# A decoder trunk on one core: float32 weights for two feature blocks, modulation blocks given out anew, a last norm by halves

## The chip, the cores and the metric

One core of a Trainium2 chip runs the whole program. The metric is device time in microseconds (us) of one execution. The engines are PE (TensorE, matmuls), DVE (VectorE), ACT (ScalarE), POOL (GpSimd) and SP (SyncE, which here only issues DMAs); each works through a queue of its own.

## What is computed

One layer on 256 tokens of width 2048, in float32:

```python
mod = (silu(c) @ w_ada + b_ada)
sh1, sc1, g1, sh2, sc2, g2 = jnp.split(mod, 6, axis=-1)
h = rms_norm(x, norm_mix) * (1.0 + sc1) + sh1
x = x + g1 * hybrid_mixer(h, w_in, w_out, ...)
h = rms_norm(x, norm_ffn) * (1.0 + sc2) + sh2
x = x + g2 * conv_glu_ffn(h, w_ffn_up, ..., w_ffn_down)
return rms_norm(x, norm_final)
```

The mixer runs retention, RWKV-7 and block-sparse attention side by side on slices of h @ w_in and multiplies the joined result by w_out. The MLP is 2 x 5632 wide, with a causal convolution of width 3 ahead of its gate.

## The kernel before

**Tiles.** Features lie on the partitions and the 256 tokens along the free axis. Every weight matrix is cut into 128x128 blocks; a block is the stationary operand of a matmul and a 128x256 feature block of the input the moving one. For exactness weights and inputs are each split into a high and a low part (`hi`, `lo`; of the inputs `hhi`, `hlo`), and a block costs three matmuls, L1226 (hi by hi), L1227 (hi by the input's low part) and L1228 (lo by hi). Eight blocks are a chunk, 24 matmuls; there are 400 chunks: "in" (w_in) 0 to 103, "out" (w_out) 104 to 135, "up" (w_ffn_up) from 136, "down" (w_ffn_down) from 312. The chunk is the only unit in which weights reach PE.

**Stream.** `stream_items` is one list of 1 MB pieces in the order in which they are used: two chunks of weights, or one modulation block (128 rows of w_ada). `pump` issues their DMAs on SP in this order, as soon as one of 3 raw slots (5 at the start: two "extra" ones) is free; later weights may also take memory that the mixer gave back, as many as `LEAD` allows at that chunk. `convert_until` takes the pieces in the same order, two chunks ahead of PE (`AHEAD`). A weight chunk is copied to `hi` by ACT (L465) and its `lo` is formed by DVE (L466); `hi` and `lo` have three buffers each (`CONVB`), so a conversion can be at most that far ahead of PE. A modulation block is one DVE instruction (L420): it multiplies the raw slot in place by `cb` (silu of c on all partitions) and sums each row into one column of `mod`; L422 or L428 adds the bias. So a raw slot with a modulation block comes free by DVE.

**Modulations.** There are 96 such blocks. Shift and gain of the first norm (32) stand among the first feature blocks of "in", g2 (16) among the last stages. The 48 between them (g1, then shift and gain of the second norm) are given out by `LATE_ADA`, in this order: the last piece of "in", four pieces of "out" of five 1 MB pieces each (the last has one), three pieces of "up". Inside each piece they are spread evenly.

```python
parts = [(win[cut[-1]:], 0)] + [(out[n:n + 5], 0) for n in range(0, 20, 5)]
parts += [(up[cut_up[g]:cut_up[g + 1]], 2) for g in range(3)]
for n, (part, after) in zip(LATE_ADA, parts):
    n_part = len(part) - after
    stream_items += mix(part[:n_part], late[:n]) + part[n_part:]
    late = late[n:]
```

`UP_BEGUN` says how many pairs of "up" tiles are begun with the first 4, 8 and 12 feature blocks of the second norm's output, before the rest of it is known.

**Order.** One Python loop over the chunks emits all instructions: conversion, hooks, the chunk's matmuls, evacuations, and `TASKS` steps of the mixer's generators. A scheduler then fixes the order of each engine's queue at build time; at run time each engine goes through its own queue and waits where an operand is not there. So a DVE instruction that is put ahead of a `lo` delays this `lo`.

**First norm.** x comes in four pieces, ACT squares them (L370), DVE adds (L374 to L376), PE averages over features (L379, `ms`), and `norm_bcast` forms m (L386), its inverse root by a bit trick and three Newton steps on DVE (`rsqrt`, L240 to L245), and spreads it by PE (L390, `rs`). `h_tile` then makes each feature block: xn (L446), `hhi` (ACT, L447), `hlo` (L448). Eight S tiles and eight W tiles of "in" take the first four feature blocks in pairs (`pair`).

**Second norm.** `evac_out` (L1066) adds gate times product to x, block by block; ACT squares it (L1079), POOL adds the squares to `acc` (L1080; DVE for the last block). `ffn_start` averages (L1084, `nps`), takes the root and multiplies; meanwhile the first eight pairs of "up" run on unnormed inputs (`xghi`, `xglo`), and `scale_early` corrects them afterwards (L1120).

**Last norm.** `evac_down` (L1167) and `norm_acc` do the same for the output, and `finish` multiplies all 16 blocks by `rs` on DVE (L1175) in five pieces and stores each from SP (L1176).

## Time and profile before

| | |
|---|---|
| times of three runs | 1270.31, 1273.58, 1273.6 us (median 1273.58) |
| profiled execution | 1276.42 us, its span 1274.6 us |
| busy: PE, DVE, ACT, POOL | 1227.2 us (96%), 1030.1 us (81%), 651.2 us (51%), 42.6 us (3%) |
| granted TensorE clock, mean | 0.987 |
| HBM read | 316.83 MB, 250 GB/s over the span |
| chain that ended last, by engine | PE 83%, DVE 7%, issue 5%, ACT 2%, DMA 1%, POOL 1% |

Span is from the first to the last instruction; some 2 us lie around it. Busy times are sums over instructions, matmuls being pipelined: the time from one matmul's start to the next is what a chunk costs, and it is read from the starts. A wait of PE that no other work fills is time lost, since PE has something to do in nearly every other microsecond. Averages over the span say little of single places; the stages below are cut at the places where the kind of work changes.

### The profile page before, as it was taken

Reading aid. Unit: us, or ns where it says so; the run is one execution under the profiler, and the core shown is the slowest. Engines: PE = TensorE matmul, PEld = TensorE weight load, DVE = VectorE, ACT = ScalarE, POOL = GpSimd, SP = SyncE. Lnnn points to the kernel's source line nnn. Section 1 sums busy time; section 2 is a strip of 40 time slices with the busy share of each in tenths; the row PEclk is TensorE's granted clock in tenths of the full one; section 3 lists DMA queues with packets and bytes.
Section 4 is the critical chain, followed back from the end, with each engine's and each line's share of the span. In section 5 each row is a group of like instructions: output and inputs, shape, how many; then the busy total and the mean of one; then the engine's idle time right before and its main releaser. Section 6 shows DMA issues by size and latency. Waiting matters only on the chain.

```text
span 1274.6 us, 25479 instructions
## 1 busy us (share of the span) xinstructions
PE 1227.2 (96%) x10608; PEld 1205.3 (95%) x10608; DVE 1030.1 (81%) x1607; ACT 651.2 (51%) x1043; POOL 42.6 (3%) x41
## 2 busy tenths in 40 slices
PE   5899999999999999899999999999999999999995
PEld 4899999989998889899999999999999999999995
DVE  6988989989988589899887999899866766666444
ACT  4354443756434534566555666666555544444441
POOL 0000000000000000600000000000000000000000
PEclk7999999999999999999999999999999999999998
DMA  9899877876654569677984565565655677767551
GB/s 387 343 365 334 341 300 273 300 261 229 230 179 166 199 240 412 241 281 254 357 308 172 193 223 200 197 232 198 216 196 188 228 263 271 285 250 288 196 199 67
DMA packets 49940, 320.58 MB, mean 252 GB/s; under 512 B 5536, under 2 KB 6048, under 8 KB 15776
## 3 DMA queue, kind: packets, MB, share of 16 engines
q1 hardware_dynamic: 48528, 315.10, 67.5%
q0 software_dynamic: 1008, 3.67, 0.8%
q8 instruction: 83, 1.36, 0.4%
q14 instruction: 33, 0.27, 0.1%
q10 hardware_dynamic: 288, 0.17, 0.1%
HBM read 316.83 MB, written 2.10 MB: 250 GB/s over the span
## 4 chain that ended last, share of the span: by engine, by line
PE 83%; DVE 7%; issue 5%; ACT 2%; DMA 1%; POOL 1%; DVEq 0%; ACTq 0%; POOLq 0%
PE mm L1226 25%; PE mm L1227 24%; PE mm L1228 24%; DVE raw L420 3%; DVE lo L466 2%; ACT hi L465 1%; PE pair L1228 1%; PE xx L787 1%; PE pair L1227 1%; PE pair L1226 1%; POOL acc L1080 1%; DMA dec<-dec 1%; PE akv L800 1%; DMA x<-xT 1%; PE cb L406 0%
## 5 line engine op out<-in xcount | busy, mean ns | idle before, releaser
L466 DVE TENSOR_TENSOR lo<-raw,hi 128x1024 fp32r<-128x1024 f32 x400 | 489.1, 1225 | 164.5 <-ACT hi L465 161.5
L465 ACT CAST hi<-raw 128x1024 fp32r<-128x1024 f32 x400 | 419.0, 1049 | 387.3 <-PE mm L1227 335.1
L1226 PE MATMUL mm<-hhi,hi 128*128 128x256 f32 x2016 | 561.0, 278 | 0.5 <-DVE proj L501 0.5
L1228 PE MATMUL mm<-hhi,lo 128*128 128x256 f32 x2016 | 559.8, 278 | 1.1 <-DVE lo L466 1.1
L1227 PE MATMUL mm<-hlo,hi 128*128 128x256 f32 x2016 | 559.8, 278 | 0.0
L1228 PEld LDWEIGHTS mm<-hhi,lo 128*128 128x128 f32 x2016 | 378.9, 188 | 2.4 <-DVE lo L466 1.9
L1226 PEld LDWEIGHTS mm<-hhi,hi 128*128 128x128 f32 x2016 | 379.4, 188 | 1.4 <-DVE proj L501 0.7
L1227 PEld LDWEIGHTS mm<-hlo,hi 128*128 128x128 f32 x2016 | 378.9, 188 | 0.9 <-issue 0.2
L420 DVE SCALAR_TENSOR_TENSOR raw<-raw,cb 128x2048 f32<-128x2048 f32 x96 | 219.8, 2290 | 6.1 <-DMA raw<-w_ada 4.9
L1226 PE MATMUL mm<-ghi,hi 128*128 128x256 f32 x704 | 194.8, 277 | 0.0
L1227 PE MATMUL mm<-glo,hi 128*128 128x256 f32 x704 | 194.8, 277 | 0.0
L1228 PE MATMUL mm<-ghi,lo 128*128 128x256 f32 x704 | 194.8, 277 | 0.0
L1226 PEld LDWEIGHTS mm<-ghi,hi 128*128 128x128 f32 x704 | 132.2, 188 | 0.0
L1228 PEld LDWEIGHTS mm<-ghi,lo 128*128 128x128 f32 x704 | 132.2, 188 | 0.0
L1227 PEld LDWEIGHTS mm<-glo,hi 128*128 128x128 f32 x704 | 132.1, 188 | 0.0
L1226 PE MATMUL mm<-mxhi,hi 128*128 128x256 f32 x256 | 72.9, 285 | 2.4 <-DVE x L1066 2.4
L1227 PE MATMUL mm<-mxlo,hi 128*128 128x256 f32 x256 | 73.1, 286 | 0.0
L1228 PE MATMUL mm<-mxhi,lo 128*128 128x256 f32 x256 | 72.5, 283 | 0.0
L1080 POOL TENSOR_TENSOR acc<-acc,nsq 128x256 f32<-128x256 f32 x28 | 36.6, 1309 | 792.9 <-ACT nsq L1079 792.5
L1226 PEld LDWEIGHTS mm<-mxhi,hi 128*128 128x128 f32 x256 | 49.0, 191 | 3.4 <-DVE x L1066 2.6
L1226 PE MATMUL pair<-hhi,hi 128*128 128x256 f32 x160 | 45.1, 295 | 6.9 <-ACT hi L465 5.0
L1228 PEld LDWEIGHTS mm<-mxhi,lo 128*128 128x128 f32 x256 | 48.8, 191 | 1.4 <-DVE lo L466 0.7
(292 smaller groups left out, 1281.8 us busy)
## 6 DMA issues: line engine op xcount, KB each, us to landing
raw<-w_ada SPq DMA_DIRECT2D x96, 1024.0 KB, 5.1
raw<-w_up SPq DMA_DIRECT2D x67, 1024.0 KB, 4.8
raw<-w_in SPq DMA_DIRECT2D x52, 1024.0 KB, 6.1
raw<-w_down SPq DMA_DIRECT2D x44, 1024.0 KB, 4.9
raw<-w_up SPq DMA_DIRECT2D x42, 512.0 KB, 8.4
raw<-w_out SPq DMA_DIRECT2D x18, 512.0 KB, 9.9
raw<-w_out SPq DMA_DIRECT2D x7, 1024.0 KB, 4.8
x<-xT SPq DMA_DIRECT2D x4, 512.0 KB, 5.6
```

Source lines behind the costliest of these rows:

```text
L420: V.scalar_tensor_tensor(raw, raw, 1.0, cb, op0=OP.mult, op1=OP.mult, accum_out=m)
L465: S.copy(flat(hi), src)
L466: V.tensor_tensor(flat(lo), src, flat(hi).bitcast(F32), op=OP.subtract)
L787: return PE.matmul(pe[e][:, o:o + 128], (Bt, Kt)[i][pb, f, sl], (At, Rt)[n][pb, f, sl], start=True, stop=True)
L800: PE.matmul(ps[:, 128 * i + 64 * e:128 * i + 64 * e + 64], xv[:, e, 128 * i:128 * i + 128], vT[:, h, 64 * hd:64 * hd + 64], start=True, st ...
L1080: (V if t == NF - 1 else G).tensor_tensor(norm["acc"], norm["acc"], sq, op=OP.add)
L1226: PE.matmul(ps, whi[:, j], hi, start=first and not (two and t % 2), stop=False, skip_group_check=two)
L1227: PE.matmul(ps, whi[:, j], lo, start=False, stop=False, skip_group_check=two)
L1228: PE.matmul(ps, wlo[:, j], hi, start=False, stop=last, skip_group_check=two)
```

## The change

- `PLAIN = 2`: the weights of the first two feature blocks are used in float32 as they lie in the raw slot. Their 4 casts and 4 `lo` are left out, and a block is one float32 matmul (L1291) with a float32 copy of the normed input (`plain`, ACT) in place of three.
- `spin`: matmuls on a zeroed tile whose result nobody reads, 12, 10, 18 and 6 of them, around the four steps of the first norm.
- First norm: the squares come behind the `cb` matmuls in the program; `rsqrt` does one Newton step on DVE and two on ACT (column by column). The modulation blocks may start only behind the first Newton step (`issue_after(seed...)`), later ones behind one of the first four xn; the first `lo` likewise.
- `LATE_ADA` becomes (8, 7, 5, 4, 0, 8, 8, 8), `UP_BEGUN` (18, 9, 7). The last piece of "in" has 10 modulation blocks fewer, "out" has 16 in place of 8, "up" 24 in place of 22.
- The load of x for the residual waits on g1's column 7 in place of its last one.
- The norms' last block: the residual sum and the squares go by halves, and the squares go to PE directly (`norm["last"]`) in place of DVE's addition to `acc`. In `finish` POOL multiplies the last four blocks by an SBUF copy of `rs` and ACT's queue stores them.
- `SMALL_PAD` 16 becomes 8, the last entry of `LEAD` (186, 1) becomes (188, 1).

```diff
-UP_BEGUN = (22, 8, 4)
+UP_BEGUN = (18, 9, 7)
+SPIN = (12, 10, 18, 6)
+PLAIN = 2
-LATE_ADA = (18, 3, 3, 2, 0, 7, 7, 8)
+LATE_ADA = (8, 7, 5, 4, 0, 8, 8, 8)
-CONST_PAD, SMALL_PAD = 32, 16
+CONST_PAD, SMALL_PAD = 32, 8
-LEAD = ((116, 0), (145, 8), (152, 6), (164, 4), (172, 3), (186, 1))
+LEAD = ((116, 0), (145, 8), (152, 6), (164, 4), (172, 3), (188, 1))
...
-        for _ in range(3):
+        if E is S:
+            half = tiny("rsh", w)
+            V.tensor_scalar(half, x, -0.5, None, op0=OP.mult)
+        for _ in range(3 if E is V else 1):
...
+        if E is S:
+            for i in range(w):
+                y1, a1 = y[:, i:i + 1], a[:, i:i + 1]
+                for _ in range(2):
+                    S.activation(a1, y1, AF.Square)
+                    S.activation(a1, a1, AF.Identity, scale=half[:, i:i + 1], bias=three_half)
+                    S.activation(y1, y1, AF.Copy, scale=a1)
...
+    def spin(n):
+        for _ in range(n):
+            tc.keep_in_program_order(PE.matmul(spin_bank[:, 0:128], idle[:, 0, 0:128], idle[:, 1, 0:128], start=True, stop=True))
...
-    ms = mean_square(XT)
+    spin(SPIN[0])
...
-    norm_scale(ms, "mix")
+    spin(SPIN[1])
+    ms = mean_square(XT)
+    norm_scale(ms, "mix", E=S, before=lambda: spin(SPIN[2]))
+    spin(SPIN[3])
...
-        V.scalar_tensor_tensor(raw, raw, 1.0, cb, op0=OP.mult, op1=OP.mult, accum_out=m)
+        with tc.issue_after((seed[:1] + scaled[:4])[-1]):
+            V.scalar_tensor_tensor(raw, raw, 1.0, cb, op0=OP.mult, op1=OP.mult, accum_out=m)
...
+            elif it[1] == "in" and it[2] < PLAIN:
+                chunks.extend((it[1], 16 * it[2] + 8 * half, flat_raw, None)
...
-                V.tensor_tensor(flat(lo), src, flat(hi).bitcast(F32), op=OP.subtract)
+                with tc.issue_after(scaled[:4][-1]):
+                    V.tensor_tensor(flat(lo), src, flat(hi).bitcast(F32), op=OP.subtract)
...
-            S.copy(x[:, 0, 0:1], mod["g1"][:, NF - 1:])
+            S.copy(x[:, 0, 0:1], mod["g1"][:, 7:8])
...
+            for h in range(2):
+                S.activation(sq[:, 128 * h:128 * h + 128], x[:, 128 * h:128 * h + 128], AF.Square)
+            norm["last"] = sq
...
+        for n, x in enumerate((norm["acc"], norm["last"])):
+            for h in range(2):
+                PE.matmul(ps[:, h:h + 1], x[:, 128 * h:128 * h + 128], K("mean"), start=(n == 0 and h == 0),
+                          stop=(n == 1), skip_group_check=True)
...
+        S.copy(rs_copy, rs[:, 0:T])
+        for a, b in ((0, 1), (1, 4), (4, 8), (8, 12)):
...
+        for a in (12, 14):
+            for t in (a, a + 1):
+                G.tensor_tensor(x1[3][:, t % 4], x1[3][:, t % 4], rs_copy, op=OP.mult)
+            S.dma_start(A["outT"][:, a:a + 2, :], x1[3][:, a % 4:a % 4 + 2])
...
+            if wlo is None:
+                PE.matmul(ps, whi[:, j], plain[0][:, k], start=first and not (two and t % 2), stop=last,
+                          skip_group_check=two)
+                continue
```

New line numbers: L420 is L455, L422 and L428 are L457 and L463, L466 is L510, L1066 is L1114, L446 and L448 are L481 and L487, L1120 is L1178, L240 to L245 are L246 to L254.

The change also moves DVE's instructions among the chunks. In the rows below a name is the tile written, then `<-` and the tiles read; `raw` with a column of `mod` is a modulation block, `lo` the low part of a weight chunk.

**First place: DVE in "out".** Before, from U (a tile of the RWKV recurrence) over the `lo` of chunks 115, 116 and 117:

```order
L953 TENSOR_TENSOR U<-u_5188,R_3478 32x512
L466 TENSOR_TENSOR lo_5438<-raw_5201,hi_5437 128x1024
L436 TENSOR_TENSOR mxlo_5183<-mix_rwkv_4909,mxhi_5182 128x4x128
L976 TENSOR_TENSOR sb_4906<-sp_5082,pcs_5194 64x4x64 x2
L1066 SCALAR_TENSOR_TENSOR x_4746<-mm_5397,mod_g_162,x_4746 128x256
L466 TENSOR_TENSOR lo_5482<-raw_5315,hi_5481 128x1024
L953 TENSOR_TENSOR U<-u_5252,R_3478 32x512
L1066 SCALAR_TENSOR_TENSOR x_4746<-mm_5467,mod_g_162,x_4746 128x256
L466 TENSOR_TENSOR lo_5511<-raw_5315,hi_5510 128x1024
```

With the change, three modulation blocks (raw_5399, raw_5433, raw_5472) stand between the `lo` of chunk 117 and these rows, which go on to the `lo` of chunk 118:

```order
L997 TENSOR_TENSOR U<-u_5142,R_3440 32x512
L1114 SCALAR_TENSOR_TENSOR x_4692<-mm_5531,mod_g_221,x_4692 128x256
L471 TENSOR_TENSOR mxlo_5137<-mix_rwkv_4855,mxhi_5136 128x4x128
L463 TENSOR_TENSOR mod_ffn_shift<-mod_ffn_shift,vec 128x1
L455 SCALAR_TENSOR_TENSOR raw_5505,mod_ffn_gain<-raw_5505,cb 128x2048
L1020 TENSOR_TENSOR sb_4852<-sp_5036,pcs_5148 64x4x64 x2
L457 SCALAR_TENSOR_TENSOR mod_ffn_gain<-mod_ffn_gain,bias_225,vec 128x1
L455 SCALAR_TENSOR_TENSOR raw_5576,mod_ffn_shift<-raw_5576,cb 128x2048
L997 TENSOR_TENSOR U<-u_5206,R_3440 32x512
L510 TENSOR_TENSOR lo_5516<-raw_5401,hi_5515 128x1024
```

Before, at most one modulation block stood between two `lo` here; now five stand between two, with the evacuation of mm_5531, whose last matmul is the last of chunk 117, among them.

**Second place: DVE in the second norm.** Before, from m on:

```order
L386 TENSOR_SCALAR m_6282<-nps_6279 128x2
L240 TENSOR_SCALAR rsy_6284<-m_6282 128x2
L241 TENSOR_SCALAR rsy_6284<-rsy_6284 128x2
L466 TENSOR_TENSOR lo_6334<-raw_5729,hi_6333 128x1024
L243 SCALAR_TENSOR_TENSOR rsa_6285<-rsy_6284 128x2
L420 SCALAR_TENSOR_TENSOR raw_6369,mod_ffn_gain<-raw_6369,cb 128x2048
L244 TENSOR_TENSOR rsa_6285<-rsa_6285,m_6282 128x2
L466 TENSOR_TENSOR lo_6376<-raw_5795,hi_6375 128x1024
L245 SCALAR_TENSOR_TENSOR rsy_6284<-rsa_6285,rsy_6284 128x2
L422 SCALAR_TENSOR_TENSOR mod_ffn_gain<-mod_ffn_gain,bias_166,vec 128x1
L243 SCALAR_TENSOR_TENSOR rsa_6285<-rsy_6284 128x2
L244 TENSOR_TENSOR rsa_6285<-rsa_6285,m_6282 128x2
```

With the change, from m on:

```order
L413 TENSOR_SCALAR m_6260<-nps_6255 128x2
L463 TENSOR_TENSOR mod_ffn_shift<-mod_ffn_shift,vec 128x1
L455 SCALAR_TENSOR_TENSOR raw_6245,mod_ffn_gain<-raw_6245,cb 128x2048
L246 TENSOR_SCALAR rsy_6262<-m_6260 128x2
L510 TENSOR_TENSOR lo_6312<-raw_5923,hi_6311 128x1024
L247 TENSOR_SCALAR rsy_6262<-rsy_6262 128x2
L457 SCALAR_TENSOR_TENSOR mod_ffn_gain<-mod_ffn_gain,bias_225,vec 128x1
L252 SCALAR_TENSOR_TENSOR rsa_6263<-rsy_6262 128x2
L510 TENSOR_TENSOR lo_6360<-raw_5996,hi_6359 128x1024
L253 TENSOR_TENSOR rsa_6263<-rsa_6263,m_6260 128x2
L455 SCALAR_TENSOR_TENSOR raw_6353,mod_ffn_shift<-raw_6353,cb 128x2048
L254 SCALAR_TENSOR_TENSOR rsy_6262<-rsa_6263,rsy_6262 128x2
```

Before, one modulation block stood in the whole chain from m to the last Newton step; now four do (two more follow these rows in the same pattern: a modulation block, a Newton row, a `lo`).

**Third place: DVE behind that chain.** Before, behind the `lo` of chunk 143:

```order
L466 TENSOR_TENSOR lo_6516<-raw_5960,hi_6515 128x1024
L448 SCALAR_TENSOR_TENSOR hlo_6465<-xn_6466,mod_ffn_shift,hhi_6464 128x256
L448 SCALAR_TENSOR_TENSOR hlo_6465<-xn_6480,mod_ffn_shift,hhi_6464 128x256
L466 TENSOR_TENSOR lo_6558<-raw_6099,hi_6557 128x1024
L1120 TENSOR_TENSOR up_6415<-up_6415,rs_ffn 128x1024
L1120 TENSOR_TENSOR up_6510<-up_6510,rs_ffn 128x1024
L466 TENSOR_TENSOR lo_6593<-raw_6100,hi_6592 128x1024
```

With the change, from the chain's last row on (the `lo` of chunk 143 is just ahead, that of chunk 144 comes 20 rows below the first one here):

```order
L254 SCALAR_TENSOR_TENSOR rsy_6262<-rsa_6263,rsy_6262 128x2
L463 TENSOR_TENSOR mod_ffn_shift<-mod_ffn_shift,vec 128x1
L455 SCALAR_TENSOR_TENSOR raw_6606,mod_ffn_gain<-raw_6606,cb 128x2048
L481 SCALAR_TENSOR_TENSOR xn_6349<-x_4689,mod_ffn_gain,rs_ffn 128x256
L481 SCALAR_TENSOR_TENSOR xn_6365<-x_4686,mod_ffn_gain,rs_ffn 128x256
L1178 TENSOR_TENSOR up_6306<-up_6306,rs_ffn 128x1024
L487 SCALAR_TENSOR_TENSOR hlo_6348<-xn_6349,mod_ffn_shift,hhi_6347 128x256
L457 SCALAR_TENSOR_TENSOR mod_ffn_gain<-mod_ffn_gain,bias_225,vec 128x1
L481 SCALAR_TENSOR_TENSOR xn_6369<-x_4686,mod_ffn_gain,rs_ffn 128x256
L455 SCALAR_TENSOR_TENSOR raw_6691,mod_ffn_shift<-raw_6691,cb 128x2048
L455 SCALAR_TENSOR_TENSOR raw_6764,mod_ffn_gain<-raw_6764,cb 128x2048
L487 SCALAR_TENSOR_TENSOR hlo_6364<-xn_6365,mod_ffn_shift,hhi_6363 128x256
```

Before, no modulation block stood between the `lo` of chunks 143 and 145; now three stand between those of chunks 143 and 144, and with them the feature blocks of the second norm, of which chunk 144 is the first to need any.

## Rows read from the trace of the kernel before

**Rows 1.** Windows: us; busy (instructions) of PE, PEld, DVE, ACT, POOL; clock, DMA share, GB/s.

```profile
23.67:56.53 32.86, 27.47 (x193) 26.57 (x194) 29.11 (x37) 10.76 (x14) 0.00 (x0) 0.87 0.90 358
...
221.90:392.60 170.70, 167.00 (x1338) 156.82 (x1337) 159.61 (x353) 92.26 (x202) 3.66 (x5) 1.00 0.66 234
392.60:536.10 143.50, 135.89 (x1293) 127.06 (x1292) 117.24 (x210) 68.84 (x132) 19.42 (x16) 0.98 0.68 261
536.10:595.00 58.90, 57.53 (x494) 57.17 (x493) 55.82 (x81) 38.04 (x88) 3.95 (x3) 1.00 0.69 250
595.00:1259.70 664.70, 664.70 (x5853) 664.70 (x5852) 497.92 (x687) 351.97 (x486) 15.36 (x14) 1.00 0.64 229
```

**Rows 2.** PE's waits: who was waited for, us in total, times, longest.

```profile
PE rs L390 <- DVE rsy L245: 9.5, 2, 7.1
...
PE pair L1226 <- ACT hi L465: 5.0, 2, 3.3
...
PE mm L1226 <- DVE x L1066: 2.4, 1, 2.4
...
PE nps L1084 <- DVE mod_ffn_shift L428: 1.3, 1, 1.3
```

**Rows 3.** Timeline of DVE, first norm: start, duration, instruction, wait ahead of it.

```profile
13.72 2.29 DVE L420 SCALAR_TENSOR_TENSOR raw<-raw,cb 128x2048 f32<-128x2048 f32 x1 [0.93 <-ACT cb L408]
...
15.93 0.15 DVE L386 TENSOR_SCALAR m<-ms 128x2 f32<-128x2 f32 x1
```

**Rows 4.** Timeline of PE, the six float32 matmuls of L675 that stand together.

```profile
243.73 1.46 PE L675 MATMUL a<-rwm,wua 96*128 96x256 f32 x6
```

**Rows 5.** Timeline of DVE in "out", end of an RWKV step.

```profile
457.44 2.28 DVE L420 SCALAR_TENSOR_TENSOR raw<-raw,cb 128x2048 f32<-128x2048 f32 x1
...
459.65 0.60 DVE L1011 SCALAR_TENSOR_TENSOR mix_rwkv<-yt,vec,rwm 128x128 f32<-128x128 f32 x2
...
461.74 0.67 DVE L953 TENSOR_TENSOR U<-u,R 32x512 f32<-32x512 f32 x1
462.34 1.20 DVE L466 TENSOR_TENSOR lo<-raw,hi 128x1024 fp32r<-128x1024 f32 x1
...
464.97 0.48 DVE L1066 SCALAR_TENSOR_TENSOR x<-mm,mod_g,x 128x256 f32<-128x256 f32 x1
```

**Rows 6.** Timeline of PE, the same place and a later one.

```profile
457.58 0.66 PE L1006 MATMUL yt<-cst,yc 128*128 128x128 f32 x4 [0.25 <-DVE yc L1002]
458.17 1.06 PE L948 MATMUL u<-sb,m 128*32 128x128 f32 x8
...
473.81 0.68 PE L921 MATMUL sp<-U,bT 32*64 32x64 f32 x16
```

**Rows 7.** Timeline of DVE, second norm, from m to the last Newton step.

```profile
541.43 0.16 DVE L386 TENSOR_SCALAR m<-nps 128x2 f32<-128x2 f32 x1 [0.69 <-PE nps L1084]
...
543.12 2.28 DVE L420 SCALAR_TENSOR_TENSOR raw<-raw,cb 128x2048 f32<-128x2048 f32 x1
...
547.70 0.16 DVE L245 SCALAR_TENSOR_TENSOR rsy<-rsa,rsy 128x2 f32<-128x2 f32 x1
```

**Rows 8.** Window behind PE's wait of 2.4 us at 524.8, columns as in rows 1.

```profile
527.40:530.90 3.50, 3.50 (x16) 3.50 (x17) 2.41 (x5) 1.58 (x3) 2.21 (x2) 0.51 0.57 239
```

**Rows 9.** DMA issues of the page: KB each, median us from issue to landing.

```profile
raw<-w_ada SPq DMA_DIRECT2D x96, 1024.0 KB, 5.1
```

**Rows 10.** DVE's waits for modulation data: us in total, times, longest.

```profile
DVE raw L420 <- DMA raw<-w_ada: 4.9, 5, 2.4
```

**Rows 11.** Timeline of the end: DVE's five multiplications and the five store DMAs.

```profile
1265.85 4.68 DVE L1175 TENSOR_TENSOR x<-x,rs 128x256 f32<-128x256 f32 x5 [1.27 <-PE rs L390]
1266.30 4.59 SPq L1176 DMA_DIRECT2D outT<-x  x5
```

**Rows 12.** Timeline of POOL: two additions of squares late in "down".

```profile
1201.19 1.40 POOL L1080 TENSOR_TENSOR acc<-acc,nsq 128x256 f32<-128x256 f32 x1 [13.83 <-ACT nsq L1079]
1216.74 0.74 POOL L1080 TENSOR_TENSOR acc<-acc,nsq 128x256 f32<-128x256 f32 x1 [14.15 <-ACT nsq L1079]
```

## What the change will do to the time, predicted blind

> **What bounds the kernel now.** I read the windows by stage first, then PE's waits, then the timelines of DVE and PE at the places where the change moves work. The windows show a PE that hardly rests: from 595 us to 1259.7 it is busy all 664.70 us, and its 5853 matmuls there stand 0.114 us apart, 2.73 us for a chunk of 24 [rows 1]. What is added or saved there on another engine costs and brings nothing; DVE is busy 497.92 of these 664.70 us. Time can be won or lost where PE waits: 170.70 - 167.00 = 3.7 us in the last part of "in", 143.50 - 135.89 = 7.6 us in "out", 58.90 - 57.53 = 1.4 us around the second norm, 32.86 - 27.47 = 5.4 us in the first feature blocks, and the first norm and the tail [rows 1]. DVE is the engine beside it: 159.61 of 170.70 us (94%) late in "in", 117.24 of 143.50 (82%) in "out", 55.82 of 58.90 (95%) around the second norm [rows 1]. The last is the stretch that a reader should keep in mind: nothing fits in there beside what there is.
>
> DVE works through its queue in the order written. In the first norm m stands behind a modulation block of 2.29 us and starts at 15.93, the moment that block ends [rows 3], although its input was ready before. So I go by the order of DVE's queue, not by its average load, and a piece of work is judged by what stands behind it.
>
> **Prices.** On DVE an instruction starts some 0.07 us before the one ahead has ended, so I count a modulation block as 2.21 us (its start to the next one's: 457.44 to 459.65), a `lo` 1.15, U 0.60, an x, xn or hlo 0.41, a mix pair 0.53 [rows 5]. The two sb are counted like two x, mxlo and yc (128x512) like U, L1178 (128x1024) like a `lo`. A small Newton row costs about 0.2 us where it waits for the one ahead and 0.07 to 0.15 where it does not: by the chain from m at 541.43 to 547.86, which is 6.43 us and holds thirteen small rows, two `lo` and one modulation block [rows 7]. With its small additions a modulation block takes 2.4 us.
>
> **The head.** Before, the first pair matmul starts at 23.67 [rows 1], behind a chain that waits 7.1 us for the root [rows 2], because a modulation block stood ahead of m and another inside the Newton rows. Now m and one Newton step come first, seven small rows or 1.4 us, and the squares behind m no longer queue among the copies of `cb`. Were m as late as `cb` (13.72, [rows 3]), shift and gain of block 0 could start at 15.1; I count 14.4, m being somewhat earlier. Two blocks and the gain's addition end near 19.1, xn and `plain` near 20.2; ACT's twelve small steps run beside the two blocks. That is 3.5 us earlier. The two plain feature blocks then cost 32 float32 matmuls. Six of them take 1.46 us with 0.38 for the last [rows 4], so 0.216 us apart, and a 128x256 product needs two instructions: 0.43 us, against 3 x 0.114 = 0.34. That makes PE's work 13.8 us in place of 10.9, but DVE and ACT lose 4 `lo` and 4 casts, which PE waited for (5.0 us on casts, [rows 2]). The slot of the first weights now comes free only when PE has read it, and DMA is at 0.90 in this stretch [rows 1], so it can bind instead. I take -3.5; ends 0 (DMA gives it all back) and -6. The spin matmuls lie in PE's wait.
>
> **Late in "in".** Ten modulation blocks leave a stretch in which DVE is 94% busy: 24 us of DVE, for 3.7 us that PE waits there. I take -2.5, ends 0 and -3.7.
>
> **"Out", the first place of the order.** DVE gets 8 blocks more, 19.5 us, and has 26.3 us idle there. By the sum they fit. But five of them stand between the `lo` of chunks 117 and 118. Count from the moment PE has finished mm_5478, in the middle of chunk 116. DVE: its evacuation 0.41, small rows 0.2 + 0.1, a block 2.21, small 0.35, yc 0.62 (3.9 us so far; PE's yt needs yc); a block 2.21, four mix pairs 2.1, U 0.6 (8.8); the evacuation of mm_5531 0.41, mxlo 0.6, small 0.1, a block 2.21, two sb 0.8, small 0.15, a block 2.21, U 0.6, the `lo` 1.2: 17.1 us. PE in the same time: 33 matmuls 3.75, yt 0.6 from 3.9 on, four u 0.5, three matmuls: 5.3; then the RWKV products between (two groups of sixteen sp, 0.68 each, eight u and yps, 1.0) and three matmuls: 7.9 [rows 6]. PE waits 9.2 us. The floor is firm: behind the evacuation of mm_5531, which cannot start before PE has ended chunk 117, stand 8.3 us of DVE against 2.6 of PE: 5.7. Behind its wait of 2.4 us for an evacuation PE had 3.5 us at a clock of 0.51, the lower of the two levels (1.2 GHz) [rows 2, 8]: 1.7 us more. I take +10.9; the ends are 5.7 and 13.3, with one late transfer more (2.4 us is the longest wait for modulation data, [rows 10]).
>
> **The second norm, places two and three.** The chain from m to the last Newton row gets three blocks and three `lo` more: by the same prices 16.3 us in place of 6.43. PE's `rs` stands 112 matmuls behind nps, 12.7 us: it waits 3.5 us, where it waited for nothing. From there to the `lo` of chunk 144 DVE has three blocks (6.6), seven xn, five hlo, two L1178 (7.2) and small rows and the `lo` (1.6): 15.4 us. PE has `rs` 0.4 and 62 matmuls 7.0, so it waits 7.5 us more at chunk 144, the first that needs these feature blocks. The next two `lo` come 4.1 and 4.9 us apart against 2.73 per chunk: 3.6 us, in which the lower clock is hidden. Less half of the 1.3 us that nps waits now [rows 2], since the halves spare DVE's addition: +13.9. Ends 7.4 (the blocks ahead of chunk 144 are run in DVE's idle time, -6.6) and 18 (data late: three raw slots hold seven blocks in a row, and each lands 5.1 us after its issue, [rows 9]).
>
> **The tail.** DVE has 12 blocks to multiply in place of 16 (4.68 us for five pieces, [rows 11]), about 1.2 us less; POOL does four beside it, and the halves save DVE's addition. One POOL pass over 128x256 took 0.74 us and another 1.40 [rows 12], the long ones beside a `lo`. At 0.74 the four are 3.0 us and end with DVE's; at 1.40 they are 5.6 and the last store goes 1.3 us later than now. I take -1.4 and as the other end +1.3. The Trainium skill ("Advanced Engine Details and Errata", Miscellaneous Facts) says that POOL shares an SBUF interface with DVE and conflicts with instructions of two SBUF inputs; DVE's multiplications here read one input from PSUM, so by it the short price holds and the term is -1.4, and without it, it would be +1.3. The `lo` with two SBUF inputs and its 1.40 agree.
>
> **Sum.** -3.5 - 2.5 + 10.9 + 13.9 - 1.4 = +17.4 us. The two blocks more in "up" and the pads: nothing, by PE's full 664.70 us. The profiled execution took 1276.4 us, 2.8 above the median of the runs, so it gives 1293.8, and from the median 1273.6 it is **1291.0**. With all low ends (-6 - 3.7 + 5.7 + 7.4 - 1.4) +2.0, with all high ends +32.6.
>
> **Rivals.** *The late-data case (slower still).* Where each of the seven blocks of the norm waits for its own transfer, 5.1 us apiece instead of 2.4 through three slots, some 8 us come on top: 1299. For it: SP issues in order and a modulation slot comes free only by DVE. Against: DVE waited for such data 4.9 us in all [rows 10], and 2.4 us would be the norm. *Averages decide (faster).* The blocks are done in the 26.3 us that DVE has idle in "out", and the waits at the three places together stay under 4.8 us; then the head, late "in" and the tail bring -3.5 - 3.7 - 1.4 = -8.6: 1265. The point at which it decides is a lead of the conversions of over 9 us, about three and a half chunks; for it speaks that PE's other waits in "out" (7.6 us, [rows 1]) could go with an earlier start, against it the three buffers of `hi` and `lo` and the evacuation of mm_5531 that holds DVE back. *Low ends (no change).* The floor of the first place, no blocks ahead of chunk 144, the full gain elsewhere: +2.0, 1275.6.
>
> **Chances.** The forecast 0.60, late data 0.14, averages 0.16, low ends 0.10. About 0.3% (3.8 us) is what a measurement of this kernel can tell from no change, so faster 0.16, same 0.10, slower 0.74. The forecast's own range is 1280 to 1301, from the ends of its two large terms with the others as taken. For 8 in 10 the range takes in part of the late data above and the low ends below, and reaches towards the averages: 1268 to 1302.
>
> **What will show it.** Right: in PE's waits an L1296 matmul that waits 6 to 11 us for a `lo` (L510) in "out" and another of 5 to 9 us around the first chunk of "up" that needs the second norm, an `rs` (L418) waiting 3 to 4 us between, and clock records at the lower level behind them; the first pair matmul near 20.3; DVE's busy share late in "in" down to about 80%. Wrong: a PE as busy as before in both places, modulation blocks there waiting for data rather than holding up a `lo`, or a first pair matmul not before 22.

## The result, and the profile after

| | before | after |
|---|---|---|
| median of four runs each (lowest to highest) | 1273.59 us (1270.31 to 1277.36) | 1293.78 us (1290.68 to 1316.81) |
| profiled execution, span | 1276.42, 1274.6 us | 1293.21, 1291.4 us |
| mean granted clock | 0.987 | 0.984 |

The ratio is 1.0153, 95% interval 1.0136 to 1.0171: the changed kernel is slower by 1.5%. Some executions of each kernel take about 20 us more (here the one of 1316.81); the ratios leave them out, and the last section shows one. The forecast was 1291.0, range 1268 to 1302; the difference of the medians is 20.2 us where +17.4 was forecast.

First the windows, cut alike in both kernels at the places the prediction speaks of. Columns as in [rows 1]; the length less PE's busy time is PE's rest. Before:

```profile
221.00:400.00 179.00, 173.92 (x1388) 162.86 (x1388) 167.66 (x370) 94.97 (x204) 3.66 (x5) 1.00 0.65 231
440.00:480.00 40.00, 39.65 (x466) 36.10 (x466) 32.31 (x62) 14.32 (x27) 0.00 (x0) 1.00 0.64 237
480.00:530.00 50.00, 47.44 (x402) 47.07 (x401) 47.48 (x77) 23.47 (x33) 12.76 (x9) 0.97 0.95 380
530.00:600.00 70.00, 68.63 (x587) 68.27 (x586) 66.20 (x93) 45.08 (x100) 8.52 (x6) 0.99 0.64 234
```

After:

```profile
221.00:400.00 179.00, 173.89 (x1396) 163.84 (x1395) 149.97 (x350) 98.17 (x223) 3.49 (x6) 0.99 0.49 176
440.00:480.00 40.00, 30.92 (x309) 28.04 (x308) 36.59 (x64) 12.40 (x22) 0.00 (x0) 0.87 0.86 312
480.00:530.00 50.00, 46.54 (x400) 45.11 (x400) 46.31 (x79) 22.65 (x34) 13.33 (x10) 1.00 0.87 331
530.00:600.00 70.00, 57.58 (x448) 56.40 (x447) 63.13 (x93) 34.49 (x82) 7.94 (x5) 0.90 0.78 300
900.00:1000.00 100.00, 100.00 (x885) 100.00 (x884) 77.26 (x118) 57.66 (x83) 0.00 (x0) 1.00 0.58 203
```

PE rests 9.1 us in place of 0.35 around the first place, 12.4 in place of 1.4 around the norm, and the granted clock there falls to 0.87 and 0.90. Late in "in" DVE has 17.7 us less to do (84% busy in place of 94%), and PE rests 5.1 us as before. Behind the norm, in the MLP, PE is busy throughout (the last row), as it was [rows 1].

PE's waits after, columns as in [rows 2]:

```profile
PE mm L1294 <- ACT silu_c L1193: 6.4, 2, 5.3
PE rs L418 <- DVE rsy L254: 5.4, 2, 3.0
PE sp L965 <- DVE U L997: 4.1, 1, 4.1
PE pair L1294 <- ACT hi L508: 4.0, 2, 3.5
PE u L992 <- DVE sb L1020: 3.6, 2, 3.4
...
PE mm L1296 <- DVE lo L510: 2.1, 4, 0.8
PE nps L1142 <- POOL acc L1133: 2.0, 1, 2.0
```

Waits for a `lo`, which I had named, are 2.1 us in all. The new waits are at sp, at u and at a product of "up" that waits for ACT; nps, the second norm's average, waits 2.0 us where it waited 1.3 [rows 2].

**Head.** DVE in the first norm, to set beside [rows 3] (start, duration, instruction, wait ahead):

```profile
13.27 0.16 DVE L413 TENSOR_SCALAR m<-ms 128x2 f32<-128x2 f32 x1 [0.70 <-PE ms L406]
...
14.35 2.29 DVE L455 SCALAR_TENSOR_TENSOR raw<-raw,cb 128x2048 f32<-128x2048 f32 x1
```

And PE, the float32 products and what follows them:

```profile
20.29 14.08 PE L1291 MATMUL pair<-plain,raw 128*128 128x256 f32 x64 [1.14 <-ACT plain L485]
34.82 0.39 PE L1294 MATMUL pair<-hhi,hi 128*128 128x256 f32 x1 [0.46 <-ACT hi L508]
```

m starts at 13.27 in place of 15.93, the first block at 14.35 (I counted 14.4), the first pair matmul at 20.29 (near 20.3). The 64 float32 instructions take 14.08 us (13.8). At the end of chunk 8 PE is 5.3 us ahead.

**First place.** DVE, where [rows 5] stood before:

```profile
457.96 2.29 DVE L455 SCALAR_TENSOR_TENSOR raw<-raw,cb 128x2048 f32<-128x2048 f32 x1 [1.33 <-DMA raw<-w_ada]
...
462.26 0.67 DVE L997 TENSOR_TENSOR U<-u,R 32x512 f32<-32x512 f32 x1
...
463.92 2.27 DVE L455 SCALAR_TENSOR_TENSOR raw<-raw,cb 128x2048 f32<-128x2048 f32 x1
...
466.13 0.85 DVE L1020 TENSOR_TENSOR sb<-sp,pcs 64x256 f32<-64x256 f32 x2
```

PE in the same place:

```profile
462.99 0.27 PE L965 MATMUL sp<-U,bT 32*64 32x64 f32 x2 [4.09 <-DVE U L997]
...
467.04 0.42 PE L992 MATMUL u<-sb,m 128*32 128x128 f32 x1 [3.36 <-DVE sb L1020]
```

U stands behind one modulation block and sb behind the next; PE's sp waits 4.09 us for U, its u 3.36 for sb. With 0.67 at yt and 0.97 behind, that is 9.1 us.

**Second norm.** DVE, where [rows 7] stood; between these two rows are three more blocks than before:

```profile
540.26 0.16 DVE L413 TENSOR_SCALAR m<-nps 128x2 f32<-128x2 f32 x1 [2.58 <-PE nps L1142]
...
557.62 0.15 DVE L254 SCALAR_TENSOR_TENSOR rsy<-rsa,rsy 128x2 f32<-128x2 f32 x1
...
557.76 2.29 DVE L455 SCALAR_TENSOR_TENSOR raw<-raw,cb 128x2048 f32<-128x2048 f32 x1
```

ACT behind it:

```profile
560.48 0.91 ACT L486 ACTIVATE hhi<-xn,mod_ffn_shift 128x256 fp32r<-128x256 f32 x2 [1.48 <-DVE xn L481]
562.94 0.51 ACT L486 ACTIVATE hhi<-xn,mod_ffn_shift 128x256 fp32r<-128x256 f32 x1 [1.55 <-DVE xn L481]
563.35 0.35 ACT L1191 COPY up<-mm 128x256 f32<-128x256 f32 x1
563.60 0.16 ACT L1193 COPY silu_c<-mm 128x1 f32<-128x1 f32 x1
```

PE:

```profile
557.83 0.71 PE L418 MATMUL rs<-cst,rsy 128*128 128x128 f32 x4 [2.96 <-DVE rsy L254]
563.82 0.58 PE L1294 MATMUL mm<-xghi,hi 128*128 128x258 f32 x1 [5.28 <-ACT silu_c L1193]
```

And the stretches from 440 to 600 us in which the granted clock is at the lower level (1.2 GHz), the first of them in the first place:

```profile
463.90:474.10 10.20, 6.09 (x61) 5.13 (x62) 10.01 (x15) 5.04 (x10) 0.00 (x0) 0.50 0.98 354
539.00:542.40 3.40, 3.40 (x18) 3.40 (x18) 2.14 (x3) 1.29 (x3) 0.00 (x0) 0.50 0.00 0
559.50:569.70 10.20, 5.88 (x27) 5.88 (x28) 10.20 (x17) 3.89 (x14) 0.00 (x0) 0.50 0.94 355
```

From m to the end of the last Newton step it is 17.5 us, where it was 6.4. Then a product of the early "up" pairs waits 5.28 us: ACT, which copies finished tiles out (L1191, L1193), has three `hhi` ahead of these copies, and they wait for DVE's xn behind modulation blocks. PE runs at a granted clock of 0.50 for 3.4 us behind its wait for nps and for 10.2 us behind its wait for `rs`; before, no part of this norm did.

**Tail.** All engines at the end, to set beside [rows 11]:

```profile
1276.97 0.28 PE L1296 MATMUL mm<-ghi,lo 128*128 128x256 f32 x1
...
1278.74 0.16 DVE L413 TENSOR_SCALAR m<-ms 128x2 f32<-128x2 f32 x1 [0.84 <-PE ms L1142]
...
1281.12 1.23 PE L418 MATMUL rs<-cst,rsy 128*128 128x128 f32 x4 [2.42 <-DVE rsy L254]
1282.44 0.37 ACT L1232 COPY rs_copy<-rs 128x256 f32<-128x256 f32 x1 [3.66 <-PE rs L418]
1282.85 3.55 DVE L1235 TENSOR_TENSOR x<-x,rs 128x256 f32<-128x256 f32 x4 [1.78 <-ACT rs_copy L1232]
1282.89 2.77 POOL L1239 TENSOR_TENSOR x<-x,rs_copy 128x256 f32<-128x256 f32 x4 [18.05 <-ACT rs_copy L1232]
1283.29 3.46 SPq L1236 DMA_DIRECT2D outT<-x  x4
```

m stands 1.77 us behind the last product (2.54 before), DVE's multiplications take 3.55 us in place of 4.68, POOL's four 0.69 each. From the last product to the end of the span it is 14.5 us, before 14.9.

To place the difference I cut both profiles at the last matmul of the same chunks. The norm's part begins behind chunk 135, the last of "out", since the wait for nps falls into chunk 136 of after. "Spacing" is what the streamed matmuls' distances (those under 130 ns) exceed 113.3 ns by, summed; it is told apart because before's profile and after's lie at different spacings in some stretches (last section). All in us, after less before:

| chunks | total | spacing | the rest | forecast |
|---|---|---|---|---|
| to 8 (head) | -5.3 | -0.8 | -4.5 | -3.5 |
| 8 to 64 | -3.1 | -3.5 | +0.5 | 0 |
| 64 to 135 (late "in", "out") | +5.9 | -0.9 | +6.8 | -2.5 + 10.9 |
| 136 to 160 (norm) | +16.8 | -0.2 | +17.0 | +13.9 |
| 160 to 399 | +2.9 | +2.3 | +0.7 | 0 |
| tail | -0.4 | 0 | -0.4 | -1.4 |
| sum | +16.9 | -3.2 | +20.1 | +17.4 |

Of the norm's 17.0 us, 11.0 are PE's rests. The two stretches of lower clock hold 45 products in 9.3 us of PE's time; at 113.3 ns they would take 5.1, so some 4 us more are an estimate of what the lower clock costs there.

### The profile page after: what moved, and what is told of

It is laid out like the page before. It is cut to its first block, busy times and chain, and to the rows that moved or that the text cites. A ratio compares the mean times of both kernels' runs of the same rounds, so it can differ in the third digit from the quotient of the medians.

```text
span 1291.4 us, 25630 instructions
## 1 busy us (share of the span) xinstructions
PE 1239.4 (96%) x10676; PEld 1216.1 (94%) x10676; DVE 1025.5 (79%) x1598; ACT 651.0 (50%) x1056; POOL 45.9 (4%) x47
## 4 chain that ended last, share of the span: by engine, by line
PE 81%; DVE 10%; DMA 4%; issue 2%; ACT 2%; POOL 1%; DVEq 0%; SPq 0%; ACTq 0%; POOLq 0%
PE mm L1294 24%; PE mm L1296 24%; PE mm L1295 24%; DMA raw<-w_ada 3%; DVE raw L455 3%; DVE lo L510 3%; ACT hi L508 1%; PE pair L1294 1%; PE pair L1296 1%; PE pair L1295 1%; PE xx L831 1%; POOL acc L1133 1%; DMA raw<-w_out 1%; PE akv L844 1%; DVE cm L859 0%
## 5 line engine op out<-in xcount | busy, mean ns | idle before, releaser
L510 DVE TENSOR_TENSOR lo<-raw,hi 128x1024 fp32r<-128x1024 f32 x396 | 484.7, 1227 | 173.8 <-ACT hi L508 169.7
L508 ACT CAST hi<-raw 128x1024 fp32r<-128x1024 f32 x396 | 414.6, 1049 | 381.6 <-PE mm L1295 332.3
L1296 PE MATMUL mm<-hhi,lo 128*128 128x256 f32 x2016 | 559.2, 278 | 2.1 <-DVE lo L510 2.1
L1296 PEld LDWEIGHTS mm<-hhi,lo 128*128 128x128 f32 x2016 | 379.1, 188 | 3.5 <-DVE lo L510 3.1
L455 DVE SCALAR_TENSOR_TENSOR raw<-raw,cb 128x2048 f32<-128x2048 f32 x96 | 220.0, 2293 | 15.1 <-DMA raw<-w_ada 14.8
L1296 PE MATMUL mm<-ghi,lo 128*128 128x256 f32 x704 | 194.8, 277 | 0.0
L1296 PEld LDWEIGHTS mm<-ghi,lo 128*128 128x128 f32 x704 | 132.2, 188 | 0.0
L1296 PE MATMUL mm<-mxhi,lo 128*128 128x256 f32 x256 | 72.4, 284 | 0.0
L1296 PEld LDWEIGHTS mm<-mxhi,lo 128*128 128x128 f32 x256 | 48.8, 191 | 0.7 <-issue 0.4
L1295 PEld LDWEIGHTS mm<-mxlo,hi 128*128 128x128 f32 x256 | 48.7, 190 | 0.6 <-issue 0.5
```

The costliest lines, as they stand in the source:

```text
L455: V.scalar_tensor_tensor(raw, raw, 1.0, cb, op0=OP.mult, op1=OP.mult, accum_out=m)
L508: S.copy(flat(hi), src)
L510: V.tensor_tensor(flat(lo), src, flat(hi).bitcast(F32), op=OP.subtract)
L1295: PE.matmul(ps, whi[:, j], lo, start=False, stop=False, skip_group_check=two)
L1296: PE.matmul(ps, wlo[:, j], hi, start=False, stop=last, skip_group_check=two)
```

## The experiments

The theory: the time goes where modulation blocks stand in a chain of DVE for which PE waits; the rivals were the number of blocks in "out", and the distance of a block from the `lo` ahead.

**a_old_late.** The change with the old table.

```diff
-UP_BEGUN = (18, 9, 7)
+UP_BEGUN = (22, 8, 4)
-LATE_ADA = (8, 7, 5, 4, 0, 8, 8, 8)
+LATE_ADA = (18, 3, 3, 2, 0, 7, 7, 8)
```

> The changed kernel with LATE_ADA and UP_BEGUN put back; head, tail and pads stay as changed. In DVE's order no two modulation blocks then stand between two lo behind the head, and one in the second norm's chain. Theory (the order of DVE's queue): the waits in "out" at 458 to 470 us (about 9 us of idle and low clock) and in the second norm (PE lost 12.3 us on the kernel before between chunks 136 and 156) go: 1293.8 - 9 - 12 - 1 = about 1271, and with the head's 5.3 us kept it is below the kernel before, 1264 to 1271. Rival (the float32 weights, the spin matmuls or the tail cost the time): it stays above 1288.

Measured: 1273.71 us (1270.14 to 1298.52), ratio 0.9985 (0.9957 to 1.0013): no difference. PE's rests are 0.4 us in 440 to 480 and 1.4 in 530 to 600, as before the change, so both losses belong to the table. But the time lies above the 1264 to 1271 expected: the head's lead, 4.9 us at chunk 8, was to stay and does not. Without spacing it is -4.3 to chunk 8, +2.1 from 64 to 135, +0.5 at the norm, -0.9 in all. With 18 blocks in the last piece of "in" PE rests 7.0 us from 221 to 400 (5.1 before): an earlier PE meets the same late DVE.

**b_new_late.** The reverse: the kernel before with the new table alone (and g1's column 7).

```diff
-UP_BEGUN = (22, 8, 4)
+UP_BEGUN = (18, 9, 7)
-LATE_ADA = (18, 3, 3, 2, 0, 7, 7, 8)
+LATE_ADA = (8, 7, 5, 4, 0, 8, 8, 8)
-            S.copy(x[:, 0, 0:1], mod["g1"][:, NF - 1:])
+            S.copy(x[:, 0, 0:1], mod["g1"][:, 7:8])
```

> The kernel before with nothing but the new LATE_ADA and UP_BEGUN (and the load of x behind g1's column 7, which the new LATE_ADA needs). Theory (the blocks given out anew make the whole loss, the head wins back a part): PE's waits grow by 20 to 25 us on the kernel before, as in the changed kernel without its head's 4.5; 1293 to 1300 where the matmuls keep their spacing of 113 ns, more where they run at 118 ns. Rival (the head's earlier start is what drives DVE into the runs): 10 to 15 us of waits, 1284 to 1289.

Measured: 1303.45 us (1296.55 to 1315.36), ratio 1.0269 (1.0197 to 1.0341). The profiled execution, the fastest of them, is 1296.55 and in the expected range, the median lies above it. Its span is 1294.8, 20.2 more than before, without spacing 24.6: that is after's 20.1 and the head's 4.5. The loss comes with the table, without the head or the tail.

**a_old_late_new_up** and **a_new_late_old_up.** Each half of the table alone in the changed kernel: the first undoes LATE_ADA only, the second UP_BEGUN only. UP_BEGUN bears on the blocks too: by the kernel's code its first entry sets the length of the first piece of "up", in which 8 blocks are mixed with 7 pieces of weights in after, 7 with 9 before. It also orders the weights of "up", and no run separates the two.

```diff
 a_old_late_new_up
-LATE_ADA = (8, 7, 5, 4, 0, 8, 8, 8)
+LATE_ADA = (18, 3, 3, 2, 0, 7, 7, 8)
...
 a_new_late_old_up
-UP_BEGUN = (18, 9, 7)
+UP_BEGUN = (22, 8, 4)
```

> The changed kernel with LATE_ADA put back and UP_BEGUN (18, 9, 7) kept. In DVE's order the run of five in "out" is gone, five blocks in the second norm's chain and a run of four behind it remain. Theory (the order): the wait in "out" goes (-9), the norm's remains (+12 to +14 on the kernel before): 1278 to 1285. Rival (it is the new LATE_ADA, in all places): 1264 to 1271, as with both put back.

> The changed kernel with UP_BEGUN put back to (22, 8, 4) and the new LATE_ADA kept. In DVE's order the run of five in "out" remains; the second norm's chain holds three blocks in place of five, and no run behind it. Theory (the order): the wait in "out" stays, the norm costs some 3 us in place of 12: 1281 to 1287. Rival (the new LATE_ADA alone makes all of it): it stays within 4 us of 1293.8.

Measured: 1303.94 us (ratio 1.0233, 1.0191 to 1.0276) and 1303.98 (1.0236, 1.021 to 1.0262). The waits fell where each table says. With the old LATE_ADA and the new UP_BEGUN only the norm rests:

```profile
440.00:480.00 40.00, 39.54 (x409) 36.73 (x409) 34.70 (x65) 14.97 (x25) 0.00 (x0) 1.00 0.74 287
...
530.00:600.00 70.00, 55.59 (x410) 54.74 (x409) 58.15 (x84) 33.12 (x81) 4.10 (x2) 0.85 0.72 271
```

With the new LATE_ADA and the old UP_BEGUN the first place does (6.6 us), and the norm less (4.3):

```profile
440.00:480.00 40.00, 33.45 (x323) 30.02 (x323) 36.54 (x66) 13.06 (x22) 0.00 (x0) 0.83 0.87 319
...
900.00:1000.00 100.00, 100.00 (x851) 100.00 (x850) 73.91 (x110) 52.96 (x76) 0.00 (x0) 1.00 0.57 199
```

Both times were missed by some 20 us. In the second the last row tells why: 851 matmuls in 100 us where after has 885, at the same granted clock of 1.00. Of its 25.7 us over before's span 20 are spacing in chunks 160 to 399. In the first spacing is 4.7 there, and without it the norm costs 20.7, 13.0 of them rests, where 12 to 14 were expected: that price left out chunk 136 with its wait for nps, and 20.5 us of this norm lie at the lower clock (13.6 in after). Its profiled execution (1297.81) is its fastest, and what the slower ones lose no trace shows.

**a_behind_lo.** Rival remedy: each late block may start only behind the last `lo` emitted.

```diff
-        with tc.issue_after((seed[:1] + scaled[:4])[-1]):
+        with tc.issue_after((seed[:1] + scaled[:4] + (lows[-1:] if p in ("g1", "ffn_shift", "ffn_gain") else []))[-1]):
             V.scalar_tensor_tensor(raw, raw, 1.0, cb, op0=OP.mult, op1=OP.mult, accum_out=m)
...
-                    V.tensor_tensor(flat(lo), src, flat(hi).bitcast(F32), op=OP.subtract)
+                    lows.append(V.tensor_tensor(flat(lo), src, flat(hi).bitcast(F32), op=OP.subtract).ins)
```

> The changed kernel, the same numbers in LATE_ADA and UP_BEGUN, but each of these 48 modulation blocks may be put into DVE's queue only behind the last lo ahead of it in the program. The runs of five and three between two lo become at most two, and the second norm's chain holds two in place of five up to the first xn. Theory (the order): most of the waits at the three places go, 1266 to 1274. Rival (averages: what counts is how many blocks a stage holds): the same blocks in the same stages, so it stays within 4 us of 1293.8.

Measured: 1309.06 us, ratio 1.0263 (1.0233 to 1.0293). Wrong, on two counts. No more than two blocks stand between two `lo`, two in the norm's chain, and the norm's rest falls only to 7.4 us, while 480 to 530 rises to 6.9. PE's waits for U and sb fall from 4.1 and 3.6 us to 1.7 and 1.8, but those for a `lo` rise from 2.1 to 5.4. And spacing takes another 24 us in the MLP (852 matmuls from 900 to 1000).

**a_same16.** The same 16 blocks in "out" and the same UP_BEGUN, but no run of five between two `lo`.

```diff
-LATE_ADA = (8, 7, 5, 4, 0, 8, 8, 8)
+LATE_ADA = (8, 8, 2, 6, 0, 8, 8, 8)
```

> The changed kernel with LATE_ADA (8, 8, 2, 6, 0, 8, 8, 8): the same 16 modulation blocks in "out", but in DVE's order no run of five any more, only two pairs elsewhere; the second norm keeps five blocks in its chain and a run of four behind it. Theory (the order): PE's idle time from 440 to 480 us, 9.1 us in the changed kernel and 0.35 before, falls under 2 us, that from 530 to 600 us stays at 10 to 14 us. Rival (averages): 6 to 9 us from 440 to 480 us as with the run, or as much more in "out" elsewhere.

Measured: 1300.75 us from two runs, ratio 1.0197 (1.0123 to 1.0271). Both windows of "out":

```profile
440.00:480.00 40.00, 39.56 (x413) 36.92 (x413) 36.40 (x68) 15.16 (x24) 0.00 (x0) 1.00 0.86 326
480.00:530.00 50.00, 42.13 (x330) 40.53 (x329) 44.97 (x76) 20.87 (x32) 13.89 (x10) 0.90 0.75 280
```

The first place's rest is gone (0.4 us), but 7.9 us appear in the next window. The same 16 blocks thus cost 8.3 us of rest in the two windows, 12.5 in after (before 2.9): their order decides where they cost, and how much. That 16 could stand in "out" for nothing this does not show; the rival's "as much more elsewhere" holds in part. DVE there:

```profile
490.16 2.28 DVE L455 SCALAR_TENSOR_TENSOR raw<-raw,cb 128x2048 f32<-128x2048 f32 x1
...
493.16 0.69 DVE L1046 TENSOR_TENSOR yc<-yc,rsy 128x512 f32<-128x512 f32 x1
```

And PE:

```profile
493.91 1.12 PE L1050 MATMUL yt<-cst,yc 128*128 128x128 f32 x4 [2.24 <-DVE yc L1046]
497.94 1.01 PE L1294 MATMUL mm<-mxhi,hi 128*128 128x256 f32 x3 [2.91 <-ACT mxhi L470]
```

A single block inside the Newton steps of the second RWKV half delays yc, and PE's yt waits 2.24 us; the mix behind it holds up mxhi for 2.91 more. So the theory had to be widened: not runs between two `lo`, but blocks in any chain of DVE that PE waits for.

**a_mid2.** A table made by that: the old UP_BEGUN, three blocks of the last piece of "in" moved on, no run, none between the norm's m and its first xn.

```diff
-UP_BEGUN = (18, 9, 7)
+UP_BEGUN = (22, 8, 4)
-LATE_ADA = (8, 7, 5, 4, 0, 8, 8, 8)
+LATE_ADA = (15, 4, 3, 3, 0, 7, 8, 8)
```

> The changed kernel with UP_BEGUN put back and LATE_ADA (15, 4, 3, 3, 0, 7, 8, 8): three blocks fewer late in "in" than before in place of ten, one or two more in "out" and "up". No run of two blocks between lo, none in the second norm's chain. Theory (late "in" holds back the head's gain because DVE is full there, and the norm's chain is better without any block): PE's waits 3 to 7 us below the kernel before; 1266 to 1271 at a matmul spacing of 113 ns in the MLP. Rival (the head's gain is lost in "out" anyway): 1272 to 1275, as with LATE_ADA put back.

Measured: 1272.79 us, ratio 0.9984 (0.9968 to 1.0000). The rests are 0.7, 2.3 and 1.8 us in the three windows from 440 on, and the losses of the change are gone. But the median is the rival's (1272 to 1275), not the 1266 to 1271 expected; without spacing the profile is 2.6 us ahead of before, where 3 to 7 were expected. Over the whole the kernel gains 0.2%, at the edge of what the comparison tells.

Rest of PE from 530 to 600, and what chunks 136 to 160 take more than before without spacing, against the blocks in the norm's chain:

| kernel | blocks from m to first xn | rest, us | 136 to 160, us |
|---|---|---|---|
| before, a_old_late | 1 | 1.4, 1.4 | 0, +0.5 |
| a_mid2 | 0 | 1.8 | +1.5 |
| a_behind_lo | 2 | 7.4 | +7.4 |
| a_new_late_old_up | 3 | 4.3 | +7.1 |
| after, a_same16 | 5 | 12.4, 12.3 | +17.0, +19.5 |
| a_old_late_new_up, b_new_late | 5 | 14.4, 16.6 | +20.7, +16.1 |

One block is free there, two or three cost 7 us and five 16 to 21, so the count orders them roughly. Differences of 2 us say nothing here: b_hiccup, b_wait and ol_plain0 below, whose code in this stretch is before's or a_old_late's, take 2.1 to 2.3 us more than before.

**ol_plain0.** What the float32 weights do, in a_old_late:

```diff
-PLAIN = 2
+PLAIN = 0
```

> The changed kernel with LATE_ADA and UP_BEGUN put back and PLAIN = 0: the first two feature blocks are cast and split as before, the rest of the new head (spin matmuls, squares, the root on two engines, order behind the seed) stays. With PLAIN = 2 PE was 4.9 us ahead of the kernel before at chunk 8. Theory (the earlier root brings 3.5 us, the plain blocks another 1 to 2 net): 3 to 4 us ahead at chunk 8. Rival (DVE's and ACT's relief is what counts, the root's chain is hidden behind the modulation blocks): under 1.5 us ahead.

Measured: one run, 1275.56 us; PE is 2.9 us ahead of before at chunk 8, with PLAIN = 2 it was 4.9. So some 2 us of the head's gain are the missing casts and `lo`, the other 3 the earlier chain; that is just under the 3 to 4 expected. In the total one run can't show it.

**b_hiccup and b_wait.** The two half tables left 20 us that no wait explained, at a spacing of 117.8 ns. Does an odd matmul in the stream cause it, or a wait? b_hiccup puts one float32 128x128 product that nobody reads into the kernel before at every 16th chunk from 160; b_wait two at every 12th from 192 to 300, of which the second reads DVE's copy of the first and so can make PE wait.

```diff
 b_hiccup
+        if c >= 160 and c % 16 == 0:
+            hic = ybank("hic")
+            with tc.issue_after(last_mm[0]):
+                tc.keep_in_program_order(PE.matmul(hic[:, 0:128], ident, ident, start=True, stop=True))
...
 b_wait
+        if 192 <= c < 312 and c % 12 == 0:
...
+            with tc.issue_after(last_mm[0]):
+                tc.keep_in_program_order(PE.matmul(hic[:, 0:128], ident, ident, start=True, stop=True))
+            V.tensor_copy(w[:, 0:128], hic[:, 0:128])
+            with tc.issue_after(last_mm[0]):
+                tc.keep_in_program_order(PE.matmul(hic[:, 128:256], w[:, 0:128], ident, start=True, stop=True))
```

> The kernel before with one 128x128 float32 matmul more (its result is read by nobody) ahead of every 16th chunk from chunk 160 on, 15 in all, some 0.2 us each. It asks why some kernels here run their MLP matmuls 113 ns apart and others 118. Theory (PE keeps one of two spacings until something breaks the stream, then either can follow): the spacing changes at some of the 15 places and holds in between, so the time is 1277 plus up to 25 us. Rival (the spacing belongs to the program's tiles): 113 ns throughout as in the profile of before, 1277.

> The kernel before with, at every 12th chunk from 192 to 300 (ten places in "up"), two 128x128 float32 matmuls more whose second waits for DVE's copy of the first: PE must wait a moment at each. The extra matmul that did not wait left the spacing at 113 ns everywhere. Theory (a wait in the stream can change the spacing, which then holds): 118 ns behind some of the ten places. Rival (the spacing is none of the waits' doing): 113 ns throughout, and 10 to 15 us for the waits.

Measured, one run each: 1276.48 us and 1297.05. In b_hiccup 900 to 1000 holds 884 matmuls and spacing costs nothing (0.05 us in chunks 160 to 399). In b_wait it costs 17.7 us there, while PE's waits for the copies come to 0.8. Its windows between the inserted pairs:

```profile
640.00:670.00 30.00, 30.00 (x267) 30.00 (x266) 23.36 (x28) 14.62 (x20) 0.00 (x0) 1.00 0.83 311
692.00:722.00 30.00, 30.00 (x257) 30.00 (x256) 26.45 (x46) 18.14 (x28) 0.00 (x0) 1.00 0.53 177
726.00:755.00 29.00, 29.00 (x258) 29.00 (x257) 25.03 (x39) 17.15 (x25) 0.00 (x0) 1.00 0.56 193
```

267 matmuls in 30 us, then 257, then 258 in 29, which is the first spacing again. It goes over at five of the ten inserted pairs (689, 723, 760, 861 and 895) and holds in between.

**a_mid2_tail.** a_mid2 with ACT's copy of `rs` behind DVE's first multiplication, which had waited for it.

```diff
-        S.copy(rs_copy, rs[:, 0:T])
         for a, b in ((0, 1), (1, 4), (4, 8), (8, 12)):
             x = x1[a // 4][:, a % 4:(b - 1) % 4 + 1]
             V.tensor_tensor(x, x, rs[:, None, 0:T].to_broadcast([128, b - a, T]), op=OP.mult)
+            if a == 0:
+                S.copy(rs_copy, rs[:, 0:T])
```

> The kernel with LATE_ADA (15, 4, 3, 3, 0, 7, 7, 8)'s neighbour of the last job, (15, 4, 3, 3, 0, 7, 8, 8), UP_BEGUN as before, new head, and in the last step the copy of rs for POOL behind DVE's first multiplication in place of ahead of it. Theory (in the changed tail DVE's first multiplication starts 0.5 us later than before because it stands behind ACT's copy): the tail from the last matmul to the end is 13.9 us in place of 14.4 (14.9 before), the whole 0.1 to 0.3% below the kernel before. Rival (the store DMAs set the end): 14.4 us as with the copy ahead.

Measured: 1271.15 us, ratio 0.9965 (0.9934 to 0.9997): 0.35% below the kernel before, and the interval just leaves 1 out. The tail is not the reason that the trace shows: from the last product to the end it takes 15.2 us where 13.9 were expected (14.8 in a_mid2). The first multiplication does come 0.5 us sooner behind `rs`, but from the first store's issue to the last landing it is now 8.3 us, where after takes 6.96 and before 7.07. With ACT's copy ahead this stretch takes 7.5 in a_mid2. So the stores set the end, as the rival said, not the multiplications.

## Why the prediction was right, and where it was not

The direction, the size and the two places were right. That the sum comes so near, +17.4 against +20.1 without spacing, is partly luck: the norm was put 3.1 us and the tail 1.0 too low, "in" and "out" together 1.6 and the head 1.0 too high. And in both places the wait that was named, for a `lo`, is not the one that came.

- *Head, -3.5.* Without spacing -4.5. The chain came as counted, to 0.1 us, and so did the float32 products. The casts and `lo` left out gave more than the float32 products take: ol_plain0 puts the net at 2 us, though PE still waits 0.46 and 3.5 us for casts behind them. That the gain would last was wrong in a_old_late, where "in" and "out" give 2.1 of 4.3 us back.
- *Late "in", -2.5.* The rest is 5.1 us before and after, although DVE fell to 84% as forecast. Chunks 65 to 80 do take 59.0 us in place of 63.1 with the same 83 products of the mixer between, but the waits only moved on (3.1 us, where it was 1.4, before a product that needs the mixer's `bd`, which DVE copies for 3.1 us at L908). A less busy engine did not shorten that chain; this is the one step that failed outright, since I argued from DVE's share there, against my own rule of the order of its queue.
- *First place, +10.9.* The waits are 9.1 us where 9.2 were forecast, but PE stops at sp and u, for U and sb, not at an L1296. I had the blocks ahead of U and sb in the count and let PE run on past them to the `lo`. The price was right since the blocks are the same; one also waits 1.33 us for its data.
- *Norm, +13.9.* It cost 17.0. `rs` waits 2.96 us (3.5). The chain is 17.5 us where 16.3 were forecast; DVE itself waits 1.56 in it, for ACT's cast (L508). The wait that follows is 5.28, not 7.5 (by the terms given, 15.4 less 7.4, it should have read 8.0), and comes right behind `rs`: I gave PE 62 matmuls to do first, but their tiles in PSUM (the memory that PE writes to) come free by ACT, whose copies queue behind `hhi`, and these behind DVE. The blocks reach PE through a third engine's queue. nps, which was to wait 0.65 us less, waits 0.7 more, for POOL's `acc`.
- *Lower clock.* This term was sized too small: I took 1.7 us in the first place and none at the norm, where it was to be hidden in the waits. The three stretches shown last 10.2, 3.4 and 10.2 us, and at the norm alone some 4 us are lost by them. Together with nps that is more than what the norm was short by.
- *Tail, -1.4.* It gained 0.4. POOL's 0.69 us each bears out the short price. The Trainium skill ("Advanced Engine Details and Errata", Miscellaneous Facts), by which POOL conflicts with DVE instructions of two SBUF inputs, agrees: DVE's multiplications beside it read one input from PSUM. The step that failed is that DVE's 1.1 us fewer would count. The stores need some 7 us from the first issue in both kernels (7.07 and 6.96), and the first one gains little because DVE's first multiplication waits for ACT's `rs_copy`.
- *Rivals.* Averages decide: its waits were to stay under 4.8 us together, and the rests are 9.1 and 12.4 us in two windows. That the order matters at an equal count a_same16 shows; whether 16 blocks could stand in "out" for nothing in some order stays open. Late data: one wait of 1.33 us in the first place, not a series of transfers. Low ends: no.
- *What I did not see at all* is the spacing, up to 24 us in a run: of the expectations missed for a_behind_lo and a_new_late_old_up it is the larger part.

## What to carry to other kernels

A free engine has no price by its share: each piece of work has the price of the chain that it is put into. One 2.2 us block between a small step and the step that PE needs costs PE up to 2.2 us, while the 23 blocks behind chunk 160 in after leave PE 0.4 us of rest in all; so list for every place the next instruction in that queue for which another engine waits, and follow queues of third engines too. A gain at the head lasts only if the next place where PE waits is not bound by something else; and two profiles should be compared by the distance of their matmuls before a difference is put down to a change.

## What the hardware showed

Matmuls of 128x256 in the stream run at one of two spacings, 113.3 or 117.8 ns, at a granted clock of 1.00 in both, for tens to hundreds of us. That is 885 or 851 in 100 us, and some 18 to 24 us over the MLP in the kernels that keep to the longer one. In before's profile it is the longer one in most of 74 to 198 us, which makes its 8th to 64th chunk 3.1 us longer than after's, although nothing is changed there (b_hiccup, with before's code in this stretch, is 2.7 us shorter too); in after's it is the longer one from 732 to 792. The spacing changes where PE's stream has a gap (0.51 us at 73.2 in before, 0.66 at 791 in after, 0.15 at 731.5): five of the ten pairs of b_wait change it, the odd matmul of b_hiccup in its one execution nowhere. Which spacing follows a wait stays open: the same inserted pair ends the longer spacing once and begins it another time. The profile of a_mid2_tail (1294.02 us) shows the longer spacing over most of the MLP:

```profile
900.00:1000.00 100.00, 100.00 (x851) 100.00 (x850) 71.90 (x103) 51.85 (x74) 0.00 (x0) 1.00 0.57 199
```

From chunk 160 to 399 its matmuls lose 21.6 us more to the spacing than before's.
